# Hybrid conv and attention layer on one core: order of the Strassen stages, banks, and where the conv taps run

## Chip, cores, metric

One Trainium2 chip, one core. The time is the device time of one execution in microseconds (us). Engines are named as in the profile: PE is TensorE's matmuls, PEld its weight loads, DVE VectorE, ACT ScalarE, POOL GpSimd, SP the queue that issues every DMA here.

## The reference, cut to what matters

The sequence has 2048 positions, the model 2048 channels, everything is float32. One input projection feeds two branches; a gated depthwise convolution (31 taps, 1024 channels) and a banded sliding-window attention (16 heads of 64, 2 key/value heads). An output projection and a layer norm end the layer.

```python
proj = einsum("bsd,de->bse", x, w_in) + b_in
c_val, c_glu, c_gate, q, k, v, a_gate = split(proj)
h = c_val * sigmoid(c_glu)
h = depthwise_causal_conv(h, conv_w, width=31) + conv_b
y_conv = silu(layer_norm(h, over channels)) * silu(c_gate)
y_attn = swa_sink_attention(q, k, v, sinks) * silu(a_gate)   # window 128
y = concat([y_conv, y_attn]) @ w_out + b_out
return layer_norm(ALPHA * x + y, ln_g, ln_b)
```

## The kernel before

**Matmuls.** Every float32 product is made of three matmuls on operands split into a high and a low part: high x high, high x low, low x high (`mm3`, L784 to L786). The high part is a copy on ACT (L132), the low part a subtraction on DVE or POOL (L135). One matmul is 128x128 by 512 columns and fills one PSUM bank of 128x512.

**Stages.** The program is a list `steps`, each step 24 such matmuls. Four chunks of 512 positions come first, 52 steps each: 8 steps for four column tiles side by side (`first`), 36 for 18 column tiles alone (`in`), 8 for the last four (`last`). They make values, gates of the GLU, queries, keys and values. The attention's work for a chunk (scores, transposes, product with the values) is spread over its steps 13 to 41. Then come the gates and the output projection, both by Strassen's scheme with 7 products in place of 8, for block 0 (chunks 0 and 1) and block 1 (chunks 2 and 3): `PRODS` gives the order of products, for the output 1, 2, 6, 5, 3, 7, 4. A product is two halves (`dp`), a half four steps, 96 matmuls into four banks. Their order is set at L670: gate block 0, gate block 1, output block 0, output block 1. The last four steps of the program are done tile by tile, each followed by its part of the norm (`tail_norm`).

**Order on the engines.** The loop over `steps` writes the program in the order in which each engine runs it; an engine takes its instructions in that order. A step first runs what `later` holds for it (postponed stores and gate products), loads and splits weights of the steps to come, loads and splits the operands of the product to come (`load_y`, `gen_y`: L557, L132, L135), writes its matmuls and evacuations, and at its end calls `run_bg(k)`: k pieces of background work. A piece is the next norm step in the deque `tq`, or, if that is empty, one tap of the depthwise convolution (L234: one DVE instruction that multiplies a shifted row by a weight and adds it to a PSUM bank `cv`). A tile of conv takes 31 taps, a chunk 8 tiles, so there are 992 taps. After the eighth tile of a chunk its layer norm over channels runs: means by a matmul against a matrix of ones (`mean_bcast`), the split of the sum of squares (tiles vsum, vs0h, vs0l for chunk 0, and so on), then scaling, swish and the store of each tile to `od`. The gate stage reloads a tile from `od`, multiplies it by the gate (`gate_done`) and stores it to `yd`, from where the output stage loads it.

**Rates.** `run_bg` takes 4 pieces a step in a chunk's steps 13 to 41 (from the loop's condition 13 <= n % 52 < 42) and 5 in its other steps; 3 or 4 by turns in the gate stages (3.5 a step); 1 in the output stages, and 3 where more than 20 pieces wait or in the last product.

**PSUM.** Eight banks: two `acc`, two `cv`, the two halves of one tile `sc` (scores), one `pt` (transposes), one `pv` (product with the values, evacuated by L369). A tile whose two halves are handed out as two banks is freed as a whole. The gate stage takes four banks of the three sides sc, pt with pv, and acc, in rotation (`gate_banks`): each half leaves out another side. The output stage takes sc, pt, pv (`right_banks`) for one half and acc, acc, cv, cv (`left_banks`) for the other. In both stages half the evacuations of a half product (in the output stage all) are written one step later, behind the first step of the next half (`late`).

**DMA.** All transfers are issued on one SP queue in the order of the program.

Of the kernel before, what the change touches and what calls it, by code (L numbers as in the profile page):

```python
# [8 lines left out]
F32 = mybir.dt.float32  # L9
# [41 lines left out]
def hybrid_layer_kernel(ctx, tc, x, xT, w_first, w_in, w_out, consts, b_out, ln_g, ln_b, out):  # L51
# [11 lines left out]
    ps_acc = ctx.enter_context(tc.tile_pool(name="ps_acc", bufs=2, space=bass.MemoryType.PSUM))  # L63
    ps_cv = ctx.enter_context(tc.tile_pool(name="ps_cv", bufs=2, space=bass.MemoryType.PSUM))
    ps_sc = ctx.enter_context(tc.tile_pool(name="ps_sc", bufs=1, space=bass.MemoryType.PSUM))
    ps_pt = ctx.enter_context(tc.tile_pool(name="ps_pt", bufs=1, space=bass.MemoryType.PSUM))
    ps_pv = ctx.enter_context(tc.tile_pool(name="ps_pv", bufs=1, space=bass.MemoryType.PSUM))

# [26 lines left out]
    def right_banks(name):  # L95
        return score_banks(name) + [ps_pt.tile([P, 512], F32, tag="pt", name=f"{name}_t"),
                                    ps_pv.tile([P, 512], F32, tag="pv", name=f"{name}_v")]

# [185 lines left out]
    def conv_var(c):  # L284
        ps = mean_bcast("vsplit", f"var{c}")
        v, y, tmp = slot(f"v{c}"), slot(f"rstd{c}"), slot(f"nt{c}")
        V.tensor_scalar(out=v, in0=ps, scalar1=EPS, scalar2=None, op0=ALU.add)
        tq.extend(rsqrt_steps(v, y, tmp))

        def fin(j):  # L290
            def f():
                a = st.pop(("conv", c, j))
                V.tensor_tensor(out=a, in0=a, in1=y, op=ALU.mult)
                u, t = half_silu_parts(a, half[:, 42 + j:43 + j], half[:, 50 + j:51 + j], f"cn{c}_{j}")
                silu_mul(u, u, t)
                store_later(od[c, 8 + j], u, 3)
            return f
        tq.extend(fin(j) for j in range(8))

# [206 lines left out]
    def gate_done(c, e, z):  # L506

        bh = half[:, 26 + e:27 + e]
        t, o = slot(f"gt{c}_{e}"), slot(f"go{c}_{e}")
        A.activation(out=t, in_=z, func=AF.Tanh, scale=0.5, bias=bh)  # L510
        A.activation(out=z, in_=z, func=AF.Identity, scale=0.5, bias=bh)
        dma(out=o, in_=od[c, e])
# [293 lines left out]

    def gate_banks(name):

        n = st["turn"] = (st.get("turn", -1) + 1) % 3

        def side(k):
            return (score_banks(f"{name}{k}") if k == 0 else
                    [ps_pt.tile([P, 512], F32, tag="pt", name=f"{name}_t"),
                     ps_pv.tile([P, 512], F32, tag="pv", name=f"{name}_v")] if k == 1 else
                    [acc_bank(f"{name}_{i}") for i in range(2)])
        return side((0, 2, 1)[n]) + side((1, 0, 2)[n])
# [51 lines left out]
    for n, s in enumerate(steps):  # L868
# [51 lines left out]
        elif s[0] == "in":  # L920
# [8 lines left out]
            if hf == 1:  # L929
                evac_in(c, t, kind, j, ps)  # L930
            run_bg(4 if 13 <= n % PER < 42 else 5)
        elif s[0] == "gate":
            _, blk, i, dp, p = s
            if p == 0:
                st["banks", dp] = gate_banks(f"gate{blk}_{i}_{dp}")
            gate_mm(n, range(4))
# [3 lines left out]
            if p == 3:  # L940
                for tp in range(2):
                    evac_gate(blk, i, dp, tp, st["banks", dp][tp])
                late = [(evac_gate, blk, i, dp, tp, st["banks", dp][tp]) for tp in (2, 3)]
            run_bg(3 + n % 2)
        else:
            _, blk, i, dp, p = s
            if i == 1 and dp == 0 and p == 0 and blk == 0:
                assert not cq and not tq
# [118 lines left out]
```

## Time and profile before

| what | value |
|---|---|
| time, median of 3 runs | 2650.05 us |
| lowest and highest of the runs | 2649.9 and 2653.05 us |
| profiled execution | 2651.39 us, its span 2649.7 us |
| DMA | 720.43 MB, mean 272 GB/s |
| HBM read, written | 564.79 MB, 153.21 MB |

How to read it: the span is cut into forty equal slices of about 66 us; a digit is the busy share of a slice in tenths, and PEclk the granted clock of TensorE in tenths.

```profile
PE   8999989999899999999999999999999999999995
DVE  3787798858887868889759999977775677987688
ACT  4577435776347765467535434544554323233321
PEclk9999999999999999999999999999999999999997
```

The chunks end in the 21st slice and the gates in the 31st; the output stages fill the rest. The chain of work that ended last names the engines that were followed back from the last instruction:

```profile
PE 60%; DVE 18%; DMA 9%; ACT 5%; issue 3%; POOL 2%; SPq 2%; DVEq 0%; ACTq 0%; POOLq 0%
```

and the conv taps are the largest group of DVE:

```profile
L234 DVE SCALAR_TENSOR_TENSOR cv<-h,cst,cv 128x512 f32<-128x512 f32 x928 | 696.0, 752 | 18.8
```

In such a row stand the line, engine, operation, the tiles out<-in with their shapes and the number of instructions; then the busy time in us and the mean of one in ns; then the idle time of the engine just ahead of them, with the releaser of most of it. (The first tap of each tile is an operation of its own, so 928 of the 992 stand here, less a few that the trace lacks.)

### The profile page before, as it was taken

The page shows a single profiled execution, that of the slowest core. Times are in us where ns is not written, and L with a number is a line of the kernel's source. Part 1 is how long each engine was busy: PE and PEld are TensorE (multiplying, and loading weights), DVE is VectorE, ACT ScalarE, POOL GpSimd, SP SyncE. Part 2 cuts the span into 40 slices and gives each one's busy share as a digit, 9 for nine tenths or more (in the row PEclk, how much of TensorE's full clock was granted, in tenths as well). Part 3 has the DMA queues.
Part 4 walks back from the last instruction along what each step waited for, and adds up shares of the span by engine and source line. Part 5 has one row for each costly group of instructions (what it writes and reads, how often), then busy time and mean ns, then how long its engine had stood idle before and what let it go on. Part 6 is the DMA issues. An engine that isn't in the chain of part 4 may idle for free.

```text
span 2649.7 us, 35489 instructions
## 1 busy us (share of the span) xinstructions
PE 2547.9 (96%) x11680; PEld 2108.7 (80%) x11680; DVE 2086.1 (79%) x3261; ACT 1303.0 (49%) x2461; POOL 972.9 (37%) x614
## 2 busy tenths in 40 slices
PE   8999989999899999999999999999999999999995
PEld 6788777887688887888887787888888888888884
DVE  3787798858887868889759999977775677987688
ACT  4577435776347765467535434544554323233321
POOL 2677824445144452426423222324222222212224
PEclk9999999999999999999999999999999999999997
DMA  7675898757986689966887767786888987899794
GB/s 278 217 260 193 287 326 277 243 177 262 339 299 249 203 296 350 328 226 224 272 274 248 246 236 268 268 292 216 292 289 289 327 304 267 305 357 341 276 319 156
DMA packets 331674, 720.43 MB, mean 272 GB/s; under 512 B 37857, under 2 KB 95329, under 8 KB 331489
## 3 DMA queue, kind: packets, MB, share of 16 engines
q1 hardware_dynamic: 331488, 718.16, 78.4%
q8 instruction: 92, 1.51, 0.2%
q14 instruction: 94, 0.76, 0.1%
HBM read 564.79 MB, written 153.21 MB: 271 GB/s over the span
## 4 chain that ended last, share of the span: by engine, by line
PE 60%; DVE 18%; DMA 9%; ACT 5%; issue 3%; POOL 2%; SPq 2%; DVEq 0%; ACTq 0%; POOLq 0%
PE in L786 6%; DVE cv L234 6%; PE in L785 6%; PE in L784 6%; PE out L785 3%; PE out L784 3%; PE out L786 3%; SPq L75 2%; PE gate_s L786 2%; PE gate_s L784 2%; PE gate_s L785 2%; DMA wl<-wlo 2%; PE out_s L784 2%; PE out_s L786 2%; PE out_s L785 2%
## 5 line engine op out<-in xcount | busy, mean ns | idle before, releaser
L135 POOL TENSOR_TENSOR wl<-wr,wh 128x1024 fp32r<-128x1024 f32 (+1 forms) x158 | 393.8, 2494 | 973.7 <-ACT wh L132 639.6
L132 ACT ACTIVATE wh<-wr 128x1024 fp32r<-128x1024 f32 (+1 forms) x436 | 455.0, 1046 | 546.5 <-DMA wr<-in_w_in_dram 81.4
L234 DVE SCALAR_TENSOR_TENSOR cv<-h,cst,cv 128x512 f32<-128x512 f32 x928 | 696.0, 752 | 18.8
L786 PE MATMUL in<-xh,wl 128*128 128x512 f32 x1280 | 502.1, 393 | 14.0 <-DMA wl<-wlo 14.0
L784 PE MATMUL in<-xh,wh 128*128 128x512 f32 x1280 | 504.1, 394 | 9.7 <-ACT xh L132 6.2
L785 PE MATMUL in<-xl,wh 128*128 128x512 f32 x1280 | 502.9, 393 | 0.0
L786 PEld LDWEIGHTS in<-xh,wl 128*128 128x128 f32 x1280 | 242.6, 190 | 67.6 <-DMA wl<-wlo 17.3
L784 PEld LDWEIGHTS in<-xh,wh 128*128 128x128 f32 x1280 | 242.5, 189 | 59.7 <-ACT xh L132 6.9
L785 PEld LDWEIGHTS in<-xl,wh 128*128 128x128 f32 x1280 | 242.4, 189 | 49.1 <-DVE xl L135 1.0
L785 PE MATMUL out<-wl,yhout 128*128 128x512 f32 x448 | 175.5, 392 | 6.4 <-DMA wl<-O_out 5.5
L132 ACT ACTIVATE yhout<-yrout 128x512 fp32r<-128x512 f32 x112 | 70.0, 627 | 216.3 <-DVE yrout L557 206.7
L786 PE MATMUL out<-wh,ylout 128*128 128x512 f32 x448 | 175.1, 391 | 0.0
L784 PE MATMUL out<-wh,yhout 128*128 128x512 f32 x448 | 166.9, 391 | 0.4 <-ACT wh L132 0.4
L135 POOL TENSOR_TENSOR plc<-pmc,phc 128x512 fp32r<-128x512 f32 x64 | 83.2, 1299 | 223.9 <-ACT phc L132 186.4
L135 DVE TENSOR_TENSOR ylgate<-yrgate,yhgate 128x512 fp32r<-128x512 f32 x112 | 109.7, 980 | 40.0 <-ACT yhgate L132 39.5
L135 DVE TENSOR_TENSOR ylout<-yrout,yhout 128x512 fp32r<-128x512 f32 x112 | 102.1, 912 | 45.0 <-ACT yhout L132 43.8
L322 ACT ACTIVATE pr<-pr,sm 128x128 f32<-128x128 f32 x256 | 99.6, 390 | 66.1 <-DVE sm L318 65.8
L132 ACT ACTIVATE yhgate<-yrgate 128x512 fp32r<-128x512 f32 x112 | 69.9, 625 | 115.3 <-DVE yrgate L557 93.9
L784 PE MATMUL gate_s<-yhgate,wh 128*128 128x512 f32 x304 | 119.0, 391 | 2.1 <-DVE g L451 1.9
L786 PE MATMUL gate_s<-yhgate,wl 128*128 128x512 f32 x304 | 119.1, 392 | 1.9 <-POOL wl L135 1.9
L785 PE MATMUL gate_s<-ylgate,wh 128*128 128x512 f32 x304 | 118.6, 390 | 0.0
L784 PE MATMUL gate<-yhgate,wh 128*128 128x512 f32 x288 | 112.8, 392 | 0.2 <-DVE g L451 0.2
(368 smaller groups left out, 5872.2 us busy)
## 6 DMA issues: line engine op xcount, KB each, us to landing
wl<-wlo SPq DMA_DIRECT2D x156, 512.0 KB, 5.1
wr<-in_w_in_dram SPq DMA_DIRECT2D x144, 512.0 KB, 5.9
yrout<-yd SPq DMA_DIRECT2D x192, 256.0 KB, 5.8
wr<-in_w_in_dram SPq DMA_DIRECT2D x320, 128.0 KB, 4.4
yrgate<-in_xT_dram SPq DMA_DIRECT2D x144, 256.0 KB, 5.1
wr<-T_gate SPq DMA_DIRECT2D x64, 512.0 KB, 6.3
wr<-T_out SPq DMA_DIRECT2D x61, 512.0 KB, 6.9
wl<-O_gate SPq DMA_DIRECT2D x56, 512.0 KB, 3.9
```

What stands on the lines that cost most here:

```text
L75: queue.append(nc.sync.dma_start(out=out, in_=in_).ins)
L132: A.activation(out=dst, in_=src, func=AF.Copy)
L135: eng.tensor_tensor(out=dst, in0=src, in1=hi.bitcast(F32), op=ALU.subtract)
L234: V.scalar_tensor_tensor(out=a if t == TAPS - 1 else acc, in0=x_, scalar=w, in1=acc, op0=ALU.mult, op1=ALU.add)
L322: A.activation(out=p3[:, u, :], in_=p3[:, u, :], func=AF.Exp, scale=HD ** -0.5, bias=sm[:, 1, u:u + 1], accum_out=sm[:, 3, u:u + 1])
L784: T.matmul(o, lh, mh, start=start, stop=False)
L785: T.matmul(o, lh, ml, start=False, stop=False)
L786: T.matmul(o, ll, mh, start=False, stop=stop)
```

## The change

1. The stages run gate block 0, output block 0, gate block 1, output block 1.
2. PSUM has one `cv` bank and two `pv` banks. The means of the conv norm use a `pv` bank.
3. The output stage takes its banks by the same rotation of three sides as the gate stage (`gate_banks` is now `four_banks`, `left_banks` is gone).
4. `run_bg` takes 3 or 4 pieces by turns in a chunk's steps 13 to 41, 3 in the gate stages, and in output block 0 1 or 2 by turns (1 in products 7 and 4).
5. With the conv of the last chunk now unfinished when gate block 1 begins, that chunk's order of conv and gate is turned round: the gate stores its tile to `od`, and the conv's last step (`cfin`, queued in the last product of gate block 1) loads it two ahead, multiplies and stores to `yd`.
6. The norm of chunk 1 (`out_norm(1)`) is queued at the start of gate block 1 (its product 1) and no longer at the start of output block 1.

```diff
-    ps_cv = ctx.enter_context(tc.tile_pool(name="ps_cv", bufs=2, space=bass.MemoryType.PSUM))
+    ps_cv = ctx.enter_context(tc.tile_pool(name="ps_cv", bufs=1, space=bass.MemoryType.PSUM))
...
-    ps_pv = ctx.enter_context(tc.tile_pool(name="ps_pv", bufs=1, space=bass.MemoryType.PSUM))
+    ps_pv = ctx.enter_context(tc.tile_pool(name="ps_pv", bufs=2, space=bass.MemoryType.PSUM))
...
-    def left_banks(name):
-        return [f(f"{name}_{i}") for i, f in enumerate((acc_bank, acc_bank, cv_bank, cv_bank))]
+    def pv_bank(name):
+        return ps_pv.tile([P, 512], F32, tag="pv", name=name)
...
     def mean_bcast(key, name):
         hi, lo = st.pop(key)
-        ps = cv_bank(name)
+        ps = pv_bank(name)
...
+        gate = {}
+
+        def load_gate(j):
+            gate[j] = slot(f"cg{c}_{j}")
+            dma(out=gate[j], in_=od[c, 8 + j])
+
         def fin(j):
             def f():
                 a = st.pop(("conv", c, j))
                 V.tensor_tensor(out=a, in0=a, in1=y, op=ALU.mult)
                 u, t = half_silu_parts(a, half[:, 42 + j:43 + j], half[:, 50 + j:51 + j], f"cn{c}_{j}")
                 silu_mul(u, u, t)
-                store_later(od[c, 8 + j], u, 3)
+                if c < NCH - 1:
+                    store_later(od[c, 8 + j], u, 3)
+                    return
+                if j + 2 < 8:
+                    load_gate(j + 2)
+                V.tensor_tensor(out=u, in0=u, in1=gate.pop(j), op=ALU.mult)
+                store_y(c, 8 + j, u)
             return f
-        tq.extend(fin(j) for j in range(8))
+        if c < NCH - 1:
+            tq.extend(fin(j) for j in range(8))
+        else:
+            st["cfin"] = [lambda: (load_gate(0), load_gate(1))] + [fin(j) for j in range(8)]
...
+        last = c == NCH - 1 and e >= 8
+        if not last:
+            o = slot(f"go{c}_{e}")
+            dma(out=o, in_=od[c, e])
 
         def f():
             silu_mul(z, z, t)
+            if last:
+                store_later(od[c, e], z, 3)
+                return
             V.tensor_tensor(out=z, in0=z, in1=o, op=ALU.mult)
             store_y(c, e, z)
...
-    prods = [(what, blk, i) for what in ("gate", "out") for blk in range(2) for i in PRODS[what]]
+    prods = [(what, blk, i) for blk in range(2) for what in ("gate", "out") for i in PRODS[what]]
...
-            run_bg(4 if 13 <= n % PER < 42 else 5)
+            run_bg(3 + n % 2 if 13 <= n % PER < 42 else 5)
...
-            run_bg(3 + n % 2)
+            if blk and i == 1 and dp == 0 and p == 0:
+                tq.extend(out_norm(1))
+            if blk and i == 4 and dp == 1 and p == 0:
+                tq.extend(st.pop("cfin"))
+            run_bg(3)
...
-                st["banks", dp] = (left_banks if dp else right_banks)(f"out{blk}_{i}_{dp}")
+                st["banks", dp] = four_banks(f"out{blk}_{i}_{dp}")
...
-                elif i == 1 and blk == 1:
-                    tq.extend(out_norm(1))
...
-            run_bg(3 if blk == 1 and i == 4 or len(tq) > 20 else 1)
+            run_bg(3 if blk == 1 and i == 4 else 1 if blk or i in (7, 4) else 1 + n % 2)
```

Where this moves instructions is shown at three places. On PE, the end of the first half of product 6 in output block 0 and the start of its second half (names: out, block, product, half, bank; `s` or a number with `s` is the tile sc, `v` the bank pv). Before:

```order
L784 MATMUL out0_6_0_v_20428<-wh339_20471,yhout0_6_7_20379 128x512
L785 MATMUL out0_6_0_v_20428<-wl339_20472,yhout0_6_7_20379 128x512
L786 MATMUL out0_6_0_v_20428<-wh339_20471,ylout0_6_7_20380 128x512
L784 MATMUL out0_6_1_0_20614<-wh340_20519,yhout0_6_0_20045 128x512
L784 MATMUL out0_6_1_1_20615<-wh340_20519,yhout0_6_0_20045 128x512
L784 MATMUL out0_6_1_2_20616<-wh340_20519,yhout0_6_0_20045 128x512
L784 MATMUL out0_6_1_3_20617<-wh340_20519,yhout0_6_0_20045 128x512
```

Now:

```order
L805 MATMUL out0_6_0_v_17607<-wh283_17651,yhout0_6_7_17556 128x512
L806 MATMUL out0_6_0_v_17607<-wl283_17652,yhout0_6_7_17556 128x512
L807 MATMUL out0_6_0_v_17607<-wh283_17651,ylout0_6_7_17557 128x512
L805 MATMUL out0_6_1_0_17799<-wh284_17701,yhout0_6_0_17206 128x512
L805 MATMUL out0_6_1_1_17800<-wh284_17701,yhout0_6_0_17206 128x512
L805 MATMUL out0_6_10_s_17801<-wh284_17701,yhout0_6_0_17206 128x512
```

The third bank of the new half is now a half of the tile sc, which the half just ended used too (out0_6_00_s); it was a cv bank, which that half did not use.

On DVE, in output block 0 behind the evacuations of the first half of product 3 (names: yrout, ylout are operands of product 7, cv3_5 is the sixth conv tile of chunk 3). Before:

```order
L557 TENSOR_TENSOR yrout0_7_3_0_21253<-yrout0_7_3_0_21253,yrout0_7_3_1_21255 128x512
L135 TENSOR_TENSOR ylout0_7_3_21289<-yrout0_7_3_0_21253,yhout0_7_3_21288 128x512
L557 TENSOR_TENSOR yrout0_7_4_0_21292<-yrout0_7_4_0_21292,yrout0_7_4_1_21294 128x512
L135 TENSOR_TENSOR ylout0_7_4_21328<-yrout0_7_4_0_21292,yhout0_7_4_21327 128x512
L557 TENSOR_TENSOR yrout0_7_5_0_21331<-yrout0_7_5_0_21331,yrout0_7_5_1_21333 128x512
```

Now:

```order
L578 TENSOR_TENSOR yrout0_7_3_0_18464<-yrout0_7_3_0_18464,yrout0_7_3_1_18466 128x512
L234 SCALAR_TENSOR_TENSOR cv3_5_18353<-h3_5_17388,cst_90,cv3_5_18353 128x512
L135 TENSOR_TENSOR ylout0_7_3_18501<-yrout0_7_3_0_18464,yhout0_7_3_18500 128x512
L234 SCALAR_TENSOR_TENSOR cv3_5_18353<-h3_5_17388,cst_90,cv3_5_18353 128x512 x4
L578 TENSOR_TENSOR yrout0_7_4_0_18504<-yrout0_7_4_0_18504,yrout0_7_4_1_18506 128x512
L234 SCALAR_TENSOR_TENSOR cv3_5_18353<-h3_5_17388,cst_90,cv3_5_18353 128x512
L135 TENSOR_TENSOR ylout0_7_4_18542<-yrout0_7_4_0_18504,yhout0_7_4_18541 128x512
```

Taps of the last chunk's conv stand between the sums and splits of the operands, where none stood.

On DVE, the split of the variance of chunk 0's conv norm (vs0l) during chunk 1's attention (ya is the evacuation of the bank pv, pmc and pmu those of the bank pt; the numbers behind ya1, pmc1 are the attention's place in the chunk). Before:

```order
L326 RECIPROCAL sm1_2_3_5758<-sm1_2_3_5758 128x4
L135 TENSOR_TENSOR vs0l_5882<-vsum0_7_5879,vs0h_5881 128x512
L369 TENSOR_TENSOR ya1_4_5902<-o1_2_0_5901,pv1_2_0_5892 64x128
L369 TENSOR_TENSOR ya1_5_5903<-o1_2_0_5901,pv1_2_0_5892 64x128
L340 TENSOR_TENSOR pmc1_2_2_5915<-pt1_2_2_5910,m_le_96 128x512
```

Now:

```order
L341 RECIPROCAL sm1_3_3_6271<-sm1_3_3_6271 128x4
L135 TENSOR_TENSOR vs0l_6324<-vsum0_7_6321,vs0h_6323 128x512
L384 TENSOR_TENSOR ya1_6_6398<-o1_3_0_6397,pv1_3_0_6388 64x128
L384 TENSOR_TENSOR ya1_7_6399<-o1_3_0_6397,pv1_3_0_6388 64x128
L355 TENSOR_TENSOR pmc1_3_2_6411<-pt1_3_2_6406,m_le_96 128x512
```

The split stands later by a quarter of the chunk's attention (the first number behind ya1 is 6 where it was 4), and still right ahead of two evacuations.

More of the change, by code (lines that the diff above doesn't have):

```diff
@@ L96, in right_banks @@
         return score_banks(name) + [ps_pt.tile([P, 512], F32, tag="pt", name=f"{name}_t"),
-                                    ps_pv.tile([P, 512], F32, tag="pv", name=f"{name}_v")]
+                                    pv_bank(f"{name}_v")]
     cst = const.tile([P, NCONST], F32, name="cst")
@@ L508, in gate_done @@
         bh = half[:, 26 + e:27 + e]
-        t, o = slot(f"gt{c}_{e}"), slot(f"go{c}_{e}")
+        t = slot(f"gt{c}_{e}")
         A.activation(out=t, in_=z, func=AF.Tanh, scale=0.5, bias=bh)
         A.activation(out=z, in_=z, func=AF.Identity, scale=0.5, bias=bh)
-        dma(out=o, in_=od[c, e])
+        last = c == NCH - 1 and e >= 8
+        if not last:
+            o = slot(f"go{c}_{e}")
+            dma(out=o, in_=od[c, e])
         def f():
             silu_mul(z, z, t)
+            if last:
+                store_later(od[c, e], z, 3)
+                return
             V.tensor_tensor(out=z, in0=z, in1=o, op=ALU.mult)
@@ L805, in gate_mm, with four_banks @@
                 mm3(st["banks", dp][tp], h, l, yh, yl, p == 0 and kk == 0, p == 3 and kk == 1)
-    def gate_banks(name):
+    def four_banks(name):
         n = st["turn"] = (st.get("turn", -1) + 1) % 3
@@ L813, in side @@
                     [ps_pt.tile([P, 512], F32, tag="pt", name=f"{name}_t"),
-                     ps_pv.tile([P, 512], F32, tag="pv", name=f"{name}_v")] if k == 1 else
+                     pv_bank(f"{name}_v")] if k == 1 else
                     [acc_bank(f"{name}_{i}") for i in range(2)])
@@ L934, in hybrid_layer_kernel @@
             if p == 0:
-                st["banks", dp] = gate_banks(f"gate{blk}_{i}_{dp}")
+                st["banks", dp] = four_banks(f"gate{blk}_{i}_{dp}")
             gate_mm(n, range(4))
```

2 lines of the change are left out of this document (removed).

## The prediction

> **What bounds the kernel now.** I read the page's span and busy times first, then the busy time cut by stage, then who waits for whom on PE.
>
> ```profile
> span 2649.7 us, 35489 instructions
> PE 2547.9 (96%) x11680; PEld 2108.7 (80%) x11680; DVE 2086.1 (79%) x3261; ACT 1303.0 (49%) x2461; POOL 972.9 (37%) x614
> ```
>
> TensorE (PE) is the bound: 102 us of the span hold no matmul, and nothing that keeps the matmul count can win more. The profiled execution took 2651.39 us, 1.34 above the median of the three timed runs and inside their spread of 3.15, so I work against 2651.39. The stretches below are cut where the first matmul of each stage starts: four chunks, gate block 0, gate block 1, output block 0, output block 1.
>
> ```profile
> core 0: us, PE busy (x) PEld busy (x) DVE busy (x) ACT busy (x) POOL busy (x), PEclk, DMA share, GB/s
> 0.00:1374.17 1374.17, 1316.54 (x6299) 1096.62 (x6299) 1063.67 (x1824) 800.41 (x1779) 637.37 (x468) 0.99 0.78 266
> 1374.17:1693.88 319.71, 311.44 (x1347) 253.96 (x1346) 290.73 (x402) 150.49 (x210) 94.23 (x39) 0.99 0.74 255
> 1693.88:2002.76 308.88, 307.10 (x1349) 252.61 (x1348) 236.34 (x303) 158.93 (x222) 84.35 (x38) 1.00 0.77 269
> 2002.76:2307.43 304.67, 304.67 (x1346) 252.22 (x1344) 219.97 (x310) 97.22 (x126) 68.97 (x28) 1.00 0.86 300
> 2307.43:2649.70 342.27, 308.18 (x1345) 253.33 (x1343) 275.35 (x425) 95.92 (x125) 88.02 (x41) 0.96 0.82 290
> ```
>
> Output block 0 is the ideal: 304.67 us with PE busy all of it, 226 ns a matmul, so a half product of 96 matmuls takes 21.7 us. Gate block 0 loses 15 us against it, gate block 1 loses 4, output block 1 nearly all of its 38 in its ending. The chunks lose 58 us of idle PE. There PE waits for:
>
> ```profile
> PE in L786 <- DMA wl<-wlo: 14.0, 7, 3.6
> PE pv L358 <- DVE ya L369: 10.6, 6, 3.3
> PE sc L307 <- DVE pr L315: 8.0, 9, 1.4
> PE pt L335 <- DVE pmu L340: 4.9, 6, 2.7
> PE in1l_s L786 <- DMA wl<-wlo: 4.7, 4, 3.0
> PE in L784 <- DVE kl L396: 3.5, 4, 2.0
> ```
>
> VectorE (DVE) causes 10.6 + 8.0 + 4.9 + 3.5 = 27.0 us of it. The waits come from order: DVE has room, but what PE wants stands behind something else. The longest pv wait:
>
> ```profile
> 574.90 0.55 PE L358 MATMUL pv<-phc,vt 128*128 128x256 f32 x1 [3.26 <-DVE ya L369]
> 572.54 0.69 DVE L135 TENSOR_TENSOR vs0l<-vsum,vs0h 128x512 fp32r<-128x512 f32 x1 [12.30 <-ACT vs0h L132]
> 574.26 0.50 DVE L369 TENSOR_TENSOR ya<-o,pv 64x128 f32<-64x128 f32 x2
> 574.78 0.69 DVE L340 TENSOR_TENSOR pmu<-pt,m_gt 128x512 f32<-128x512 f32 x1
> ```
>
> DVE stood 12.30 us at the variance split of the conv norm, the evacuations ya behind it, and PE could not reuse the one pv bank. A wait also leaves PE on half clock; the third number from the end is the granted clock:
>
> ```profile
> 113.00:119.80 6.80, 6.00 (x19) 0.50 0.98 339
> 573.80:580.60 6.80, 5.70 (x20) 0.50 0.76 301
> 625.00:628.40 3.40, 3.40 (x15) 0.50 1.06 395
> 1447.60:1451.00 3.40, 3.40 (x9) 0.50 0.79 266
> ```
>
> Half of each window is lost: 3.4, 3.4 and 1.7 us behind the pmu wait and two of the ya waits.
>
> **The change part by part.** Work is moved, hardly any is added: 992 conv taps, the norms and 28 products as before. Counted from the order of DVE (cut where the second product of a stage splits its first operand), the taps stand as follows: chunks 774, now 717; gate block 0 184, now 144; output block 0 none, now 68; gate block 1 34, now 63.
>
> ```profile
> L234 DVE SCALAR_TENSOR_TENSOR cv<-h,cst,cv 128x512 f32<-128x512 f32 x159 | 119.5, 751 | 2.8
> L627 DVE SCALAR_TENSOR_TENSOR zl<-zl,mv,g 128x512 f32<-128x512 f32 x8 | 8.1, 1017 | 1.0 <-DMA zl<-zd 1.0
> L627 DVE SCALAR_TENSOR_TENSOR xn<-xn,mv,g 128x512 f32<-128x512 f32 x8 | 7.8, 1008 | 0.0
> L628 DVE SCALAR_TENSOR_TENSOR zl<-zl,w,b 128x512 f32<-128x512 f32 x8 | 7.5, 939 | 0.1
> L628 DVE SCALAR_TENSOR_TENSOR xn<-xn,w,b 128x512 f32<-128x512 f32 x8 | 5.8, 740 | 0.0
> ```
>
> At 0.751 us a tap, DVE's load becomes: chunks -43 us; gate block 0 291 - 30 = 261; output block 0 220 + 51 = 271; gate block 1 236 + 22 + 29 (the norm of chunk 1, 8.1 + 7.8 + 7.5 + 5.8, moved there from output block 1) = 287. All stay under the 305 that PE needs.
>
> *Chunks.* The second pv bank takes away the ya wait; in the case above the next PE demand on DVE is the transpose bank, whose pmu ends under 1 us after the ya. I take 9 of the 10.6, and the two half-clock windows (5 us). The other 16.4 us of DVE waits and the 3.4 us window at 113 shrink with the rate. The 43 us leave the attention steps. Over four stretches of these (90 to 330, 440 to 620, 820 to 1010, 1130 to 1300):
>
> ```profile
> sum 780.00, PE 754.40 PEld 638.12 DVE 611.88 ACT 527.06 POOL 453.03; mean PE 188.60 PEld 159.53 DVE 152.97 ACT 131.76 POOL 113.26
> ```
>
> DVE is idle for 168 us there; 43 more is a quarter more room. I take 40% of the 19.8, so 8. Together **-22**, with bounds 0 and -35.5 (all 27.0 and all 8.5). The single cv bank costs nothing: one conv writes it, and its next user is the next conv on the same engine.
>
> *Gate block 0.* PE waited little for DVE here:
>
> ```profile
> PE gate_t L784 <- DVE g L493: 0.9, 1, 0.9
> PE gate_v L784 <- DVE g L451: 0.8, 1, 0.8
> PE gate_s L784 <- DVE g L451: 0.4, 1, 0.4
> PE gate_s L786 <- POOL wl L135: 1.9, 1, 1.9
> ```
>
> With 2.1 us to win, and the tap-laden half products (28 and 31 us of DVE by the order, before 24 and 31) still above 21.7, I take **0**, bounds -2 and +4.
>
> *Output block 0.* Here the change pays. Before, the two halves of a product used disjoint sets of four banks, so an evacuation had 21.7 us to spare. Now three pairs rotate, and the third bank of a half is the first of the half before: the order asks for it three to seven matmuls past the boundary, 0.5 to 1.4 us. How late DVE may be shows at the end of product 7 (PE first, then DVE):
>
> ```profile
> 2263.91 0.39 PE L784 MATMUL out_s<-wh,yhout 128*128 128x512 f32 x1
> 2264.56 0.68 DVE L451 TENSOR_TENSOR U<-U,out 128x512 f32<-128x512 f32 x1
> 2267.98 0.67 DVE L451 TENSOR_TENSOR U<-U,out 128x512 f32<-128x512 f32 x1
> ```
>
> The second bank came free at 2268.65, 4.7 us past the boundary; by the new order PE wants it after 0.7. It cost nothing before, and 4 us now. More taps make DVE later. Durations in this block:
>
> ```profile
> L135 DVE TENSOR_TENSOR ylout<-yrout,yhout 128x512 fp32r<-128x512 f32 x56 | 53.9, 964 | 27.8 <-ACT yhout L132 27.2
> L557 DVE TENSOR_TENSOR yrout<-yrout,yrout 128x512 f32<-128x512 f32 x48 | 41.5, 865 | 6.0 <-DMA yrout<-yd 5.5
> L440 DVE BATCH_NORM_STATS2 bn<-xn 128x6 f32<-128x512 f32 x28 | 18.4, 681 | 0.0
> L451 DVE TENSOR_TENSOR xn<-xn,out 128x512 f32<-128x512 f32 x22 | 14.2, 681 | 11.6 <-PE out L786 11.6
> ```
>
> Between the evacuations of the two halves of product 3 stand 17 taps, 5 splits, 5 sums, 5 statistics and 4 adds: 17 x 0.751 + 5 x (0.964 + 0.865 + 0.681) + 4 x 0.681 = 28.0 us (27 with overlaps), for 21.7 of PE. Summed alike, seven of the 14 halves exceed 21.7, by 6.9, 1.5, 3.6, 1.5, 5.2, 2.9 and 2.8: 24.4 us. The first is passed by: there PE's order leaves the bank until 44 matmuls (10 us) on. Of the other 17.5 I allow 1.4 us of margin to each of six, and take **+9**, bounds 0 (PE is never reached) and +24.4. *Gate block 1*: halves of 24 and 27 us against a margin of 4, **+1**, bounds 0 and +6. *Output block 1*: the norm of chunk 1 is gone, so two halves exceed (3.6 and 4.6), the second beside an ending in which PE waits anyway:
>
> ```profile
> PE out L785 <- DMA wl<-O_out: 5.5, 1, 5.5
> ```
>
> **+2**, bounds 0 and +8. That ending is the same work and stays.
>
> *DMA.* Eight gate stores replace eight conv stores and eight reloads the eight of the gate stage; the moved stages take their loads along on the one SP queue, and chunk 3's products are stored over 80 us before product 6 loads them. **0.**
>
> Sum: -22 + 0 + 9 + 1 + 2 = -10, so 2641.4 profiled and **2640 us** timed.
>
> A rule weighed: the Trainium skill, "TensorE: Matmul & The Clock Gate", section "HAM oscillation — how this bites in real kernels", lets the clock fall only after PE idles for more than about 3.4 us. Of the rows above, the window at 1447.6 stands behind a wait of 1.9 us (gate_s for POOL), so this trace does not agree. By the rule the new waits cost no clock and the sum stays; by the row each wait of 2 us or more can cost 1.7 us.
>
> **The rivals.**
> 1. *The banks are the bound of the output stages (slower).* If DVE has no margin, output block 0 pays all 24.4, output block 1 its 2, and five waits above 2.5 us pay 1.7 of clock each, 8.5: with -22 and +1 from the rest that is +14, 2664 timed. For it: the 4.7 us lateness existed before the taps came in. Against it: a late DVE finds its inputs ready and catches up. It decides once the output stages wait more than 22 us.
> 2. *The gain is hidden (no change).* Chunk 1 is followed by 18.7 us of weight waits on DMA (14.0 + 4.7 over all chunks); an earlier PE only meets the same transfers earlier. If they take 12 of the 22, the sum is +2 or so: 2650.
> 3. *The second bank does nothing.* The wait moves to the transpose bank, still single, and behind the same split. Then the 14 us of bank and clock shrink to 4 and the sum is 0: 2650. The page named above says in the same section that double-buffered PSUM gave one kernel no further gain; here the pv row speaks against that.
>
> **How the numbers follow.** About 0.2% (5.3 us) can be told from no change, so faster is below 2644.7 and slower above 2655.4. Chances: forecast 0.46 (its own range 2626 to 2646), rival 1 0.24, rival 2 0.20, rival 3 0.10. One part in ten of each case spills over its border: faster 0.46, same 0.30, slower 0.24. The range 2618 to 2664 runs from nearly the whole chunk gain with a cheap output stage to rival 1.
>
> **What would show it.** Right: the first gate matmul starts near 1352 instead of 1374; the row of pv waiting for ya is gone; output block 0 takes about 314 us, with waits for DVE adds a few matmuls past the boundaries of products 6, 3 and 7. Wrong: the same start of the gates with new pt or wl waits (rivals 2, 3), or output blocks beyond 325 us with half-clock windows in them (rival 1), or output block 0 still at 305 with the chunk gain kept, near 2630.

## The result, and the profile after

The changed kernel takes **2716.77 us** (median of 4 runs), the kernel before 2651.55 in the same session: a ratio of **1.0251** (95% interval 1.0238 to 1.0263). It is 65 us slower where 10 us faster was forecast. The page of the changed kernel begins:

```profile
span 2711.8 us, 35518 instructions
PE 2567.8 (95%) x11680; PEld 2121.6 (78%) x11680; DVE 2129.6 (79%) x3261; ACT 1305.0 (48%) x2461; POOL 982.6 (36%) x614
```

PE has the same 11680 matmuls and is busy 19.9 us longer, on half clock for a part of them; the other 42 us of the 62.1 by which the span grew are idle PE. By stage, cut at the first matmul of each, now in the order chunks, gate 0, output 0, gate 1, output 1:

```profile
core 0: us, PE busy (x) PEld busy (x) DVE busy (x) ACT busy (x) POOL busy (x), PEclk, DMA share, GB/s
0.00:1378.50 1378.50, 1317.00 (x6296) 1099.95 (x6297) 1056.90 (x1758) 800.11 (x1777) 642.82 (x466) 0.98 0.77 265
1378.50:1711.03 332.53, 313.89 (x1350) 255.70 (x1349) 283.69 (x378) 152.29 (x213) 89.74 (x39) 0.98 0.72 247
1711.03:2036.52 325.49, 311.60 (x1346) 254.53 (x1344) 272.76 (x391) 98.84 (x127) 73.15 (x30) 0.98 0.80 282
2036.52:2365.71 329.19, 312.94 (x1350) 255.83 (x1349) 260.69 (x355) 152.12 (x212) 86.89 (x38) 0.98 0.75 259
2365.71:2711.80 346.09, 312.36 (x1345) 255.60 (x1343) 255.58 (x383) 101.61 (x134) 90.00 (x42) 0.96 0.78 278
```

| stage | before | after | forecast of the difference | measured |
|---|---|---|---|---|
| chunks | 1374.2 | 1378.5 | -22 | +4.3 |
| gate block 0 | 319.7 | 332.5 | 0 | +12.8 |
| output block 0 | 304.7 | 325.5 | +9 | +20.8 |
| gate block 1 | 308.9 | 329.2 | +1 | +20.3 |
| output block 1 | 342.3 | 346.1 | +2 | +3.8 |

The waits of PE that answer to those shown of before:

```profile
PE out_s L805 <- DVE xn L466: 15.3, 4, 5.1
PE pt L350 <- DVE pmu L355: 13.5, 7, 6.9
PE gate_s L805 <- DVE g L466: 11.6, 2, 6.9
PE in L805 <- ACT wh L132: 10.5, 3, 8.2
PE in L807 <- DMA wl<-wlo: 9.8, 5, 3.6
```

The wait of pv for ya (10.6 us) is gone; the wait of pt for pmu grew from 4.9 to 13.5, and one for the weight splits on ACT is new. Below them stand the waits for late evacuations (xn in the output, g in the gates).

In this program PE fills a bank again only after the copy that empties it (its evacuation). The slowest halves of gate block 0 (its fifth, sixth and last) show what a late evacuation is:

```profile
1466.12:1493.18 27.06, 23.46 (x99) 17.98 (x97) 26.81 (x33) 11.55 (x17) 14.34 (x9) 1.00 0.57 191
1493.18:1523.50 30.32, 25.24 (x96) 19.68 (x97) 27.16 (x39) 12.73 (x19) 6.61 (x3) 0.89 0.48 165
1679.74:1711.03 31.29, 24.41 (x98) 19.68 (x97) 31.04 (x41) 12.62 (x18) 8.86 (x4) 0.89 0.63 223
```

DVE (fourth column) is busy for 26.81 of 27.06, 27.16 of 30.32 and 31.04 of 31.29 us. In the fifth and the last DVE, not PE, is the bound, though the stage's DVE is idle for 49 us in all. The sixth holds no tap; PE waited in it for ACT (2.3, 1.2 and 1.1 us) and POOL (1.7 us), and part of it ran at half clock (0.89 on average).

### The profile page after: what moved, and what is told of

It is laid out like the page before. It is cut to its first block, busy times and chain, and to the rows that moved or that the text cites. A ratio compares the mean times of both kernels' runs of the same rounds, so it can differ in the third digit from the quotient of the medians.

```text
span 2711.8 us, 35518 instructions
## 1 busy us (share of the span) xinstructions
PE 2567.8 (95%) x11680; PEld 2121.6 (78%) x11680; DVE 2129.6 (79%) x3261; ACT 1305.0 (48%) x2461; POOL 982.6 (36%) x614
## 4 chain that ended last, share of the span: by engine, by line
PE 58%; DVE 19%; DMA 11%; ACT 4%; issue 3%; POOL 2%; SPq 2%; DVEq 0%; ACTq 0%; POOLq 0%
PE in L807 7%; PE in L805 7%; PE in L806 7%; DVE cv L234 5%; PE out_s L805 2%; PE out_s L807 2%; PE out_s L806 2%; PE gate_s L805 2%; PE gate_s L806 2%; PE gate_s L807 2%; PE out L806 2%; PE out L807 2%; PE out L805 2%; PE gate L805 2%; PE gate L807 2%
## 5 line engine op out<-in xcount | busy, mean ns | idle before, releaser
L135 POOL TENSOR_TENSOR wl<-wr,wh 128x1024 fp32r<-128x1024 f32 (+1 forms) x158 | 387.5, 2454 | 1047.0 <-ACT wh L132 655.1
L135 DVE TENSOR_TENSOR ylgate<-yrgate,yhgate 128x512 fp32r<-128x512 f32 x112 | 101.7, 909 | 58.6 <-ACT yhgate L132 54.4
L805 PE MATMUL out_s<-wh,yhout 128*128 128x512 f32 x304 | 121.5, 400 | 19.7 <-DVE xn L466 15.3
L805 PE MATMUL gate_s<-yhgate,wh 128*128 128x512 f32 x304 | 120.7, 397 | 14.4 <-DVE g L466 11.6
L805 PE MATMUL gate<-yhgate,wh 128*128 128x512 f32 x304 | 120.0, 395 | 2.7 <-ACT g L132 2.3
L806 PE MATMUL out_s<-wl,yhout 128*128 128x512 f32 x304 | 120.5, 396 | 0.0
L807 PE MATMUL out_s<-wh,ylout 128*128 128x512 f32 x304 | 120.3, 396 | 0.0
L807 PE MATMUL gate<-yhgate,wl 128*128 128x512 f32 x304 | 118.7, 396 | 1.4 <-POOL wl L135 1.4
```

The lines of the kernel that those rows point to most:

```text
L135: eng.tensor_tensor(out=dst, in0=src, in1=hi.bitcast(F32), op=ALU.subtract)
L805: T.matmul(o, lh, mh, start=start, stop=False)
L806: T.matmul(o, lh, ml, start=False, stop=False)
L807: T.matmul(o, ll, mh, start=False, stop=stop)
```

## The experiments

All times are medians in us; the ratio is to the kernel before in the same session, with its 95% interval. The stages are from the one profiled execution. The same program text in the chunks ended at 1378.5 to 1386.4 in four kernels and at 1369.7 to 1374.2 in three, so a difference of some 8 us in a single stage of the chunks is not read as an effect.

| kernel | time | ratio | chunks | gate 0 | gate 1 | output 0 | output 1 |
|---|---|---|---|---|---|---|---|
| e1_pv | 2655.43 | 1.0030 (1.0019 to 1.0041) | 1370.1 | 327.7 | 309.4 | 304.6 | 341.6 |
| e2_rate | 2691.96 | 1.0165 (1.0145 to 1.0185) | 1387.6 | 342.6 | 319.0 | 304.7 | 341.5 |
| e3_rot | 2673.39 | 1.0097 (1.0077 to 1.0117) | 1372.7 | 319.5 | 311.0 | 315.1 | 352.0 |
| e4_order | 2705.51 | 1.0221 (1.0203 to 1.0240) | 1381.7 | 337.7 | 321.9 | 314.5 | 348.5 |
| e5_rates | 2701.51 | 1.0202 (1.0181 to 1.0222) | 1371.7 | 330.9 | 321.4 | 328.8 | 351.4 |
| e6_tile | 2663.88 | 1.0061 (1.0046 to 1.0076) | 1369.7 | 319.1 | 309.6 | 312.8 | 348.6 |
| e7_vsplit | 2673.50 | 1.0097 (1.0074 to 1.0119) | 1387.5 | 327.9 | 309.5 | 305.0 | 340.5 |
| e8_notap | 2678.70 | 1.0116 (1.0099 to 1.0132) | 1386.4 | 308.8 | 319.1 | 315.1 | 349.8 |
| e9_both | 2659.29 | 1.0037 (1.0023 to 1.0051) | 1373.0 | 327.9 | 312.0 | 304.7 | 341.8 |
| e10_rate5 | 2679.20 | 1.0114 (1.0099 to 1.0129) | 1414.1 | 314.7 | 306.3 | 304.7 | 341.4 |
| e11_atile | 2702.58 | 1.0199 (1.0184 to 1.0214) | 1382.9 | 332.0 | 327.1 | 317.5 | 342.5 |
| e12_order5 | 2698.20 | 1.0185 (1.0170 to 1.0200) | 1421.0 | 318.9 | 309.3 | 308.4 | 340.2 |
| e13_seven | 2649.64 | 1.0005 (0.9991 to 1.0019) | 1365.2 | 327.3 | 309.7 | 304.7 | 339.2 |
| e14_seven | 2666.14 | 1.0069 (1.0043 to 1.0094) | 1376.8 | 328.5 | 310.0 | 304.7 | 340.8 |
| e16_pvvs | 2666.29 | 1.0071 (1.0043 to 1.0099) | 1376.9 | 330.7 | 311.1 | 304.7 | 340.6 |
| e17_vsts | 2646.81 | 1.0001 (0.9986 to 1.0016) | 1366.8 | 319.0 | 309.6 | 304.7 | 338.9 |

### The second pv bank alone: e1_pv

To the kernel before:

```diff
-    ps_cv ... bufs=2
+    ps_cv ... bufs=1
-    ps_pv ... bufs=1
+    ps_pv ... bufs=2
-        return [... (acc_bank, acc_bank, cv_bank, cv_bank) ...]
+        return [... (acc_bank, acc_bank, cv_bank, pv_bank) ...]
-        ps = cv_bank(name)     # in mean_bcast
+        ps = pv_bank(name)
```

> The kernel before with the second pv bank alone (one cv bank, means in a pv bank, the output stage still with two disjoint sets of four banks). If the bank does what the forecast said, the row of pv waiting for ya goes, no other row grows by more than 3 us, and the chunks end near 1360 (14 us earlier): 2636. If the wait only moves to the transpose bank behind the same variance split, pt waiting for pmu grows from 4.9 us to 12 or more and the chunks still end between 1370 and 1378: 2645 to 2655.

Measured: 2655.43, no gain but 7 us lost. The waits of PE in this kernel:

```profile
PE pt L338 <- DVE pmu L343: 15.3, 8, 3.5
PE gate_s L787 <- DVE g L454: 9.4, 2, 7.0
```

The ya row is gone and pmu is at 15.3: the wait moved to the next bank. Its longest, 3.5 us, still stands behind the same split (vs0l), the second, 3.1 us, behind the last part of the norm. And gate block 0 grew by 8. There the banks show: counted from the trace, 757 taps run before the first gate matmul, where the kernel before has 774. The 17 others (12.8 us of DVE at 0.75) fall on the gate blocks. No run separates the single cv bank from the means' move to a pv bank.

### Lower rate alone: e2_rate

```diff
-            run_bg(4 if 13 <= n % PER < 42 else 5)
+            run_bg(3 + n % 2 if 13 <= n % PER < 42 else 5)
-            run_bg(3 + n % 2)      # gate stages
+            run_bg(4)
```

> The kernel before with the lower conv rate in the chunks alone (3 and 4 by turns; the gate stages take 4 a step, so that the conv still ends in time). If room on DVE is what the chunks lack, they end 8 us earlier (1366) and the time is about 2645. If the lower rate only moves the conv's norm to another place, where its activations stand ahead of the weight splits, waits of PE for ACT wh and xh of 10 to 17 us appear in the chunks, as in the changed kernel, and the chunks end between 1375 and 1390: 2652 to 2668.

Measured: 2691.96, 44 us slower, more than either theory said. The chunks ended 13 us later; the wait that grew there is one for DVE (kl, the low part of the keys, 12.3 us for 3.5), while ACT wh was 1.3, so the second theory had the chunks' size and not the engine. The other 33 us are in the gates, where DVE was busy 311.96 us in block 0 (290.73 before); the higher rate there (4 for 3.5) is a part of this edit.

### The rotation alone, and with more margin: e3_rot, e6_tile, e11_atile

e3_rot is the kernel before with the rotation in its output stage (`gate_banks` in place of `left_banks` and `right_banks`). The margin is the time by which an evacuation may be late before PE asks for the bank again. e6_tile adds the following to it, and e11_atile adds the same to the changed kernel:

```diff
-        for kk in range(2):
-            ...
-            for tp in tps:
+        for tp in tps:
+            for kk in range(2):
...
-                late += [(evac_out, blk, i, dp, tp) for tp in range(4)]
+                for tp in range(2):
+                    evac_out(blk, i, dp, tp)
+                late += [(evac_out, blk, i, dp, tp) for tp in (2, 3)]
```

> The kernel before with the rotation of three sides in the output stage alone (no taps there). If the short margin of the rotation is the cause of the loss, even with DVE at 220 us in output block 0 some evacuations come late: waits of PE for DVE xn and U of 8 to 25 us in the two output blocks, 2658 to 2675. If the order of the stages and the taps are needed for it, the output blocks stay within 3 us of 304.7 and 342.3: 2648 to 2655.

> The kernel before with the rotation in the output stage, as in e3_rot, but with each step's matmuls bank by bank and the first two banks evacuated at once. The shared pair is then done 12 to 18 matmuls ahead of the boundary and asked for 12 behind it, 5 to 7 us of margin for 0.5. If the short margin made the loss of e3_rot, at least half of its 25 us goes: 2650 to 2662. If not, 2668 or more.

> The changed kernel with the output stage's matmuls bank by bank and its first two banks evacuated at once, as in e6_tile. If the short margin of the rotation is a part of its loss, the two output blocks together lose 10 to 20 us of their 672 and the time is 2695 to 2708. If DVE's load alone decides, less than 6: 2710 or more.

Measured: the rotation alone costs 25 us, 10.4 in output block 0 and 9.7 in output block 1, without one tap in either. In e3_rot's output blocks PE now waits:

```profile
PE out_s L784 <- DVE xn L451: 13.4, 4, 4.7
PE out L784 <- DVE xn L451: 5.8, 3, 2.1
PE out_t L784 <- DVE U L451: 3.6, 1, 3.6
```

None of these rows is in the kernel before. With the longer margin it is 16 instead of 25 us (just short of the half that was asked for), and the changed kernel gains 14 (ratio 1.0251 to 1.0199), 11.6 of it in the two output blocks. The short margin is a part of the loss, not all of it.

### The order of the stages: e4_order, e12_order5

e4_order is the changed kernel with the line that sets `prods`, the place of `out_norm(1)` and the gate rate as before. e12_order5 is the kernel of e1_pv with `run_bg(5)` in all chunk steps and, alone of the rest of the change, the new order and `out_norm(1)` in gate block 1; its output stage keeps two disjoint sets of banks.

> The changed kernel with the old order of stages (gate, gate, output, output), the norm of chunk 1 back in output block 1 and the gate rate of before. If the alternating order is the cause, gate block 1 falls back to about 309 and the time is within 10 us of 2655. If the rotation is, gate blocks are near the old 320 and 309 but the output blocks keep 10 to 25 us of waits for DVE: 2665 to 2680. If neither alone, 2700 or more remain.

> The order of stages alone: gate, output, gate, output with the second pv bank, two disjoint sets of banks in the output stage and the rate of e10_rate5, by which all taps are done when output block 0 begins. If the order is harmless, the time is that of e10_rate5 and the 7 us of e1_pv, within 6 us. If alternating the stages costs by itself (norms and operand sums in other places), 10 us or more above that.

Measured: going back to the old order takes the ratio from 1.0251 to 1.0221, 8 of the 65 us (the same edit, with the old gate rate beside it); gate block 1 is at 321.9, not 309. The new order together with the bank costs 19 us against e10_rate5, 12 beyond the 7 of the bank alone, spread over the chunks (6.9, within their scatter) and the three stages behind them (4.2, 3.0, 3.7). So 8 to 12 us, if the two add, and no single place.

### The rates: e5_rates, e10_rate5

e5_rates is the changed kernel with 4 in the chunks and 3 or 4 in the gates, as before. e10_rate5 is the kernel before with `run_bg(5)` in every step of the chunks.

> The changed kernel with the conv rates of before in the chunks (4 a step) and in the gate stages (3 and 4 by turns). If the lower rates are the larger cause (they push the conv's norms to later places and taps into the gates), the chunks end near 1372, gate block 0 takes 320 to 328, and the time falls by 25 to 40 us against the changed kernel: 2675 to 2692. If the order of the stages and the rotation are the whole cause, the time stays within 12 us of it: 2705 or more.

> The kernel before with 5 pieces of background work in every step of the chunks, the opposite of the change. If the gate stages lose time to taps that fall on their halves, gate block 0 falls from 320 to 306 to 312, and if the chunks have the room the time is 2634 to 2646. If the taps then make PE wait in the chunks' attention, the chunks end 10 us or more later (1384) and the time is 2650 to 2665.

Measured: the old rates take the ratio from 1.0251 to 1.0202, 13 us, under the 25 expected; gate block 0 stays at 330.9, as it does with the banks alone (327.7 in e1_pv). More taps in the chunks do take time from the gates (5.0 and 2.6 us), but the chunks lose 40, a wait of 11.7 us for ya among them:

```profile
PE pv L358 <- DVE ya L369: 21.9, 7, 11.7
PE in L784 <- ACT wh L132: 11.7, 4, 4.3
```

So 3.5 and 5 taps a step are both worse than 4. DVE's load alone would not give that; the place of something could, which the next three kernels take up.

### Where the norm of the conv falls: e7_vsplit, e9_both, e17_vsts

Each edit of the rate also moves the conv's norm, since it follows the last tap. Its last part (conv<-conv,rstd) began, for chunks 0 to 2, at 618, 1025 and 1414 us before, and at 650, 1070 and 1510 in the changed kernel. e7_vsplit moves the norm and nothing else; e9_both moves POOL's jobs for the Strassen weights by as much; e17_vsts does as e9_both, with the split moved in chunks 0 and 1 only.

```diff
-                    split_sum("vsplit", st["vsum"], f"vs{c}")
-                    later.append((st["n"] + 3, lambda: conv_var(c)))
+                    later.append((st["n"] + 3, lambda: split_sum("vsplit", st["vsum"], f"vs{c}")))
+                    later.append((st["n"] + 6, lambda: conv_var(c)))
...
-        n = 10 + 6 * j      # e9_both and e17_vsts only
+        n = 13 + 6 * j
```

> The kernel before with the split of the variance written three steps later (and what follows it as well), no other edit. If DVE standing at that split, not the single bank, makes the waits for ya and pmu, the row of pv waiting for ya falls from 10.6 us below 4 without pmu growing, DVE's waits at vs0l and its sisters (12.3 us the longest) go, and the chunks end 5 to 12 us earlier: 2638 to 2646. If the wait only moves on, 2648 or more.

> The kernel of e7_vsplit (variance split and the norm behind it three steps later) with the jobs of POOL that sum and split weights for the Strassen stages (tb, tl) also three steps later, so that the norm stands to them as before. If the 25 us of e7_vsplit come from the norm's DVE instructions meeting POOL's, the group conv<-conv,rstd of chunk 0 runs at 0.7 us each again instead of 1.5, the chunks end at 1380 or earlier and the time is 2648 to 2662. If the later place itself costs it, whatever POOL does, the chunks end near 1387 and the time stays at 2667 or more.

> The kernel before with the variance split of the first two chunks three steps later and POOL's weight jobs three steps later, the other norms left where they were. Chunk 2's norm then stands in gate block 0 as before, so if the 8 us that gate block 0 lost in e9_both came from that norm's place, gate block 0 is back at 318 to 322 and the time is 2645 to 2652. If it is not, 2655 or more. This kernel is also the control of the next.

Measured: three steps (16 us) cost 25 us, most of it in the chunks (13) and gate block 0 (8). In e7_vsplit the timeline of DVE, then of POOL, from 633 us on reads:

```profile
634.40 6.19 DVE L293 TENSOR_TENSOR conv<-conv,rstd 128x512 f32<-128x512 f32 x4
640.52 1.75 DVE L162 SCALAR_TENSOR_TENSOR gu<-gt,gu 128x512 f32<-128x512 f32 x1
642.20 1.74 DVE L293 TENSOR_TENSOR conv<-conv,rstd 128x512 f32<-128x512 f32 x1
```

```profile
634.94 1.74 POOL L135 TENSOR_TENSOR tlgate<-tbgate,thgate 128x512 fp32r<-128x512 f32 x1
636.75 1.62 POOL L598 TENSOR_TENSOR tbgate<-tbgate,tbgate 128x512 f32<-128x512 f32 x1
638.34 1.71 POOL L135 TENSOR_TENSOR tlgate<-tbgate,thgate 128x512 fp32r<-128x512 f32 x1
640.00 1.72 POOL L598 TENSOR_TENSOR tbgate<-tbgate,tbgate 128x512 f32<-128x512 f32 x1
```

The two engines take turns: four multiplications take 6.19 us where six took 3.69 in the kernel before, at 1024.98, with POOL idle. The evacuation behind them kept PE waiting for 11.2 us. With POOL's jobs out of the way the row of this group (ns, least, median and most) is back; first e7_vsplit, then e9_both:

```profile
L293 DVE TENSOR_TENSOR conv<-conv,rstd x8: 677/1431/1775, 634.4 to 647.3; 128x512 f32<-128x512 f32 x8
```

```profile
L293 DVE TENSOR_TENSOR conv<-conv,rstd x8: 676/677/678, 625.4 to 630.8; 128x512 f32<-128x512 f32 x8
```

and the chunks end at 1373.0 for 1387.5. In e17_vsts gate block 0 is back at 319.0 as well, so its 8 us came from the place of chunk 2's norm. Its time is that of before: the DVE waits that it takes away in the chunks aren't seen in the median.

### The taps in the stages: e8_notap

```diff
-                else:
+                elif st["n"] < OUT0 or t == TAPS - 1:
                     V.scalar_tensor_tensor(...)
```

> The changed kernel without the conv taps that fall in the gate and output stages (all but the first and the last of a tile are left out, their turns stay empty, so all else keeps its place). If DVE's load in the halves is what PE waits for, the halves of 27 to 31 us in the gates and output block 0 fall to 22 to 25 and the two gate blocks and output block 0 together lose 35 us or more of their 987: 2665 to 2682. If the margin of the banks or the order costs it whatever DVE has to do, they lose less than 15: 2700 or more.

e8_notap leaves out 261 of the 992 taps, so its conv is not complete; it shows what the rest takes without them.

Measured: the ratio falls from 1.0251 to 1.0116, 36 us; gate block 0 falls by 23.7, output block 0 by 10.4, gate block 1 by 10.1, together 44 of 987. The three slow halves shown above become

```profile
1473.94:1496.95 23.01, 22.78 (x99) 18.32 (x98) 16.22 (x19) 11.58 (x17) 12.57 (x7) 1.00 0.73 255
1496.95:1521.09 24.14, 22.06 (x98) 17.95 (x96) 22.38 (x32) 9.38 (x15) 4.98 (x2) 1.00 0.51 183
1673.41:1695.17 21.76, 21.76 (x98) 18.02 (x96) 12.73 (x18) 12.36 (x18) 5.00 (x3) 1.00 0.85 303
```

The sixth half had no tap to lose. It holds 4.8 us less of DVE because DVE did that work earlier, with fewer taps ahead of it.

What is left in output block 0 (315.1) is what the rotation alone costs in e3_rot (also 315.1).

### The bank without the split, and more margin in the gates: e16_pvvs, e13_seven, e14_seven

e16_pvvs is e17_vsts with the second pv bank. e13_seven is e1_pv with the gate's halves on seven banks (each string names the banks of one half, `sc` for two, and a mean in the stages takes a spare pv bank as well); e14_seven has both.

```diff
+    SEVEN = ("acc acc pv pt", "pv sc acc", "acc pv pt pv", "acc sc acc", "pv pt pv acc", "acc sc pv",
+             "pt pv acc acc", "pv sc pt", "pv acc acc pv", "pt sc pv")
...
-                st["banks", dp] = gate_banks(f"gate{blk}_{i}_{dp}")
+                st["banks", dp] = seven_banks(f"gate{blk}_{i}_{dp}")
```

> The kernel of e17_vsts with the second pv bank (means in it, one cv bank). If the bank pays once the variance split no longer stands ahead of the transpose bank, the waits for ya go and pmu does not grow, and the chunks end 6 us or more ahead of e17_vsts (1367 or earlier). If the bank is worth nothing in the chunks even so, they end within 4 us of it.

> The kernel of e1_pv with the gate stage's halves taking four of seven banks, so that only the last bank of a half is shared, with the first of the half before: done 18 matmuls (4 us) ahead of the boundary and asked for 18 behind it. If the margin of the gate's rotation is what makes halves of 24 to 31 us there, gate block 0 falls from 328 to 318 or less and the time to 2640 to 2648. If DVE's load in these halves decides, whatever the margin, it stays within 5 us: 2650 to 2660.

> The kernel of e13_seven with the chunk edits of e16_pvvs. If both parts hold and add, the chunks end at 1367 or earlier, gate block 0 takes 318 or less, and the time is 2632 to 2643, under both kernels. If either is worth nothing, 2646 or more.

Measured: with the split out of its way the bank still doesn't pay; e16_pvvs is 19 us slower than e17_vsts (10 in the chunks, 11.7 in gate block 0). Its ya row is down to 2.5 us from 6.1 in e17_vsts, but pmu is up from 1.5 to 6.0, so the wait moves on even where the split is out of the way. Seven banks leave gate block 0 at 327.3: its margin of 8 us changes nothing where DVE has 27 us to do in 22. The 6 us between e13_seven and e1_pv lie mostly in the chunks, whose text is the same. e14_seven wins nothing either. No kernel here beats the one before.

## Why the prediction was wrong

Three steps failed: that the second pv bank and the room on DVE win 22 us in the chunks (the waits moved to other places instead), that the loaded halves of the gate blocks cost no more than before (33.1 us more), and that the rotation with taps costs 9 us in output block 0 (20.8). Stage by stage:

- **Chunks, -22, measured +4.3.** Of the step "the second pv bank takes away the ya wait" the first half held. "The next PE demand on DVE is the transpose bank, whose pmu ends under 1 us after the ya" was read in the right row with the wrong conclusion: what ends 1 us later also waits nearly as long. That is rival 3, and e1_pv shows it. In the changed kernel the longest wait for pmu (6.9 us at 599.4 us) is not behind the split at all: three subtractions of chunk 0's norm (L269) took 5.09 us from 588.12 on, beside POOL, and four taps followed. "The single cv bank costs nothing" did not hold for the bank edits together: 17 taps left the chunks. "40% of the 19.8, so 8" for the lower rate treated room on DVE as what decides; e2_rate, e7_vsplit and e9_both show that the lower rate moves the norm, and where it meets POOL it costs more than the room is worth. The ACT wait has the same root: in the changed kernel the activations of chunk 1's norm follow each other from 1071 us on, ahead of the weight split for chunk 3's early steps, and PE stood 8.2 us (the longest of the ACT wh row).
- **Gate block 0, 0 with bounds -2 and +4, measured +12.8.** The hand sums for the new kernel were right: 28 and 31 us of DVE in two halves. They were then argued away with the 24 and 31 of before, and that comparison is the step that failed. In the trace of before no half of this stage holds more than 23.48 us of DVE (the sixth), and the last took 22.34 us with 22.09 of DVE; first these two, then the last half of e1_pv:

```profile
1488.20:1514.97 26.77, 24.12 (x97) 18.80 (x96) 23.48 (x30) 10.70 (x15) 8.90 (x4) 0.94 0.54 187
1671.54:1693.88 22.34, 21.98 (x97) 17.87 (x96) 22.09 (x30) 11.23 (x16) 5.57 (x2) 1.00 0.82 270
```

```profile
1667.20:1697.80 30.60, 23.59 (x98) 19.09 (x97) 29.90 (x43) 13.85 (x21) 8.89 (x3) 0.89 0.65 224
```

  From before to now the last half grew by 9.0 us, the fifth by 5.3 and the sixth by 3.6; the other eleven together lost 5. The last half was nearly as long with the bank edits alone. e8_notap shows that the taps make these halves long, e13_seven that margin is no cure.
- **Output block 0, +9 with bounds 0 and +24.4, measured +20.8.** The mechanism was right, the size wrong: half of it is the rotation without a tap (e3_rot, 10.4), half the taps (e8_notap, 10.4). The allowance of "1.4 us of margin to each of six" was too kind, since evacuations stood 4.7 us behind the boundary already before.
- **Gate block 1, +1, measured +20.3.** Here the bound of +6 failed. The norm of chunk 1, the conv norm of the last chunk and its taps came together. The taps are half of it (e8_notap, 10.1). The other half stands where the last chunk's conv norm runs. Two halves there (a half without a wait takes 21.8 us) took, first in the changed kernel, then in e8_notap:

```profile
2266.68:2292.85 26.17, 23.09 (x99) 18.25 (x98) 22.42 (x22) 13.16 (x20) 16.45 (x10) 1.00 0.77 251
2314.60:2343.94 29.34, 24.61 (x97) 19.78 (x96) 22.35 (x32) 13.58 (x19) 4.81 (x2) 0.88 0.63 229
```

```profile
2230.84:2257.00 26.16, 23.08 (x100) 18.25 (x99) 22.46 (x22) 13.13 (x20) 16.44 (x10) 1.00 0.73 251
2278.75:2307.68 28.93, 24.21 (x98) 19.53 (x97) 22.29 (x32) 13.62 (x19) 4.81 (x2) 0.88 0.66 235
```

  None of them holds a tap. The two halves that hold chunk 1's norm took 21.8 and 22.2 us, so that norm is not it. No run moves the last chunk's norm alone.
- **Output block 1, +2, measured +3.8**, and **DMA, 0**: held. The larger row of weight loads in the chunks fell from 14.0 to 9.8 us.
- **The clock.** "By the row each wait of 2 us or more can cost 1.7" was too broad, but no length of a single wait divides the rows either. In the changed kernel the stretches of 3.4 us behind waits of 1.93, 2.14, 2.57, 2.70 and 2.98 us had full clock; those behind 3.26, 3.53, 3.67, 4.06 and 6.88 us had 0.50 to 0.56, and so had those behind 2.76 us (at 111.9) and 2.29 us (at 1503.2, with waits of 1.1 and 1.7 us just ahead). Four of them, behind the waits of 2.98, 3.53, 2.76 and 2.29 us (the granted clock is third from the end):

```profile
1765.80:1769.20 3.40, 3.36 (x15) 1.00 0.36 143
1827.30:1830.70 3.40, 3.36 (x8) 0.50 0.73 237
112.40:115.80 3.40, 2.89 (x12) 0.50 1.02 374
1503.20:1506.60 3.40, 3.37 (x8) 0.50 0.32 67
```

  The Trainium skill ("TensorE: Matmul & The Clock Gate", section "HAM oscillation — how this bites in real kernels") puts the limit at gaps of about 3.4 us. Most of these rows fit it; those behind 2.29 and 2.76 us do not, nor does the row at 1447.6 of before, behind waits of 0.2 and 1.85 us with two matmuls between. What else decides stays open.
- **The rivals.** Rival 1 named the right place, with 2664; the gate blocks and the chunks were missing from it. Rival 3 came true beside it. Rival 2 did not: the weight waits on DMA shrank. The two that did were not alternatives, as the chances had them, but added: the chunk gain gone, and 57.7 us of loss in the four stages.

The parts don't add up one by one. Alone, the rotation costs 25 us, the bank 7 and the order about 10; the rates cost 44 in e2_rate and give back 13 in e5_rates. The taps, the banks and the norms draw on one thing, DVE's time in single halves, so their costs overlap; the rotation takes margin, and in the chunks ACT's order and the meeting with POOL come beside it. How much of the 65 us each has in the full change stays open.

## What to carry to other kernels

Sum the in-order engine's work for each stretch between two moments at which the bound engine depends on it, and enter every excess; an average of 85% over the stage hides stretches of 100%. A second buffer behind a blocked engine only shows the next buffer. And a rate of background work sets where the work behind it lands: look at what that meets before counting the room.

## What the runs showed that was not expected

A DVE operation on 128x512 with two inputs in SBUF can take four times as long beside POOL's. In the kernel before, 550 such TENSOR_TENSORs that overlap no POOL TENSOR_TENSOR take at most 0.70 us; of 152 that do, some take up to 2.91, and together they take 114 us more than at 0.69. Those with an input in PSUM take at most 0.69 either way, and the conv taps (one input in PSUM) at most 0.76. The changed kernel's 165 take 133 us more, which is 19 of the 43.5 us by which its DVE is busy longer for the same 3261 instructions. The Trainium skill says so ("SBUF — State Buffer", section "SBUF: two separate sides"): for a DVE operation with two SBUF inputs and a POOL operation that reads SBUF the shared ports are an exclusive lock, held for the whole instruction. The trace agrees, with the alternation in e7_vsplit as its plainest picture. It means that a conv tap, which reads PSUM, is cheaper to place beside POOL's work than a norm step of the same length.
